# A two-layer trunk on one core: POOL's and PE's side work issued at other places

## The chip, the core and the metric
The kernel runs on one core of a Trainium2 chip. The metric is device time in microseconds (us), median over runs, lower is better. The engines named are PE (TensorE, matrix multiplies), DVE (VectorE), ACT (ScalarE), POOL (GpSimd) and SP (SyncE, which issues all of the DMAs spoken of here). PEld is PE's weight load. L442 means line 442 of the kernel before; where a line of the changed kernel is meant, the text says so.

## The reference
Two layers, sequence 1024, width 1024, float32 in and out. Cut to what matters:

```python
for layer in range(2):
    h = rmsnorm(x, pre_mix_g[layer])
    # layer 0: conformer conv (GLU, width-31 depthwise conv, LayerNorm, swish)
    #          beside an RG-LRU block, joined by one output projection
    # layer 1: mLSTM matrix memory, chunkwise, with a running-max stabiliser
    h = ab_mixer(h, ...) if layer == 0 else mlstm_mixer(h, ...)
    x = x + rmsnorm(h, post_mix_g[layer])
    h = swiglu(rmsnorm(x, pre_ffn_g[layer]), w_gate, w_up, w_down)   # 1024 -> 2816 -> 1024
    x = x + rmsnorm(h, post_ffn_g[layer])
```

## The kernel before
The sequence is held as two halves, A and B, of T = 512 columns. Every product of two float32 matrices is done as three matmuls on high and low parts (`mm3`, L126 to L128); a weight tile `raw` is loaded, cast to its high part on ACT and subtracted to its low part on DVE (`split`, L131 and L132). So a PE step waits for: a load, a cast on ACT, a subtraction on DVE.

The feed-forward part is a Strassen-Winograd scheme over quarters. `phase0` makes the hidden values of half A (blocks `EARLY`, then the last one, `LATE`). `down_first` does the first product of the down projection (`d1`: 11 steps, weight tiles `r20a` in layer 0, `r21a` in layer 1). `phase1` does the gate and up products of both halves jointly over 11 blocks m: for each block it needs joint weights t1 to t4, sums and differences of the raw weight tiles `ri` and `rj`, one set for gate ("g") and one for up ("u"). POOL makes them in `prep1a` (four operations for each kind, L448 to L451; tiles `t14…`, `t23…`), ACT and DVE split them in `prep1b` (`whit2…`, `wlot2…`, and `b22…` for the plain quarter). Before the loop over m, `phase1` also finishes the sums of the activations of half B (`xa…`, `xs…`, `xk…`, L374 to L388, then splits to `xs1…`, `xs2…`, `xa22…`). `down_sums` makes the sums t1 to t4 of the down weights on POOL (11 blocks, four operations and four stores to DRAM each). `phase2` does the six other products of the down projection in the order a12, s4, s2 (with t2), s1 (t1), s3 (t3), a22 (t4).

The order is set by code and a scheduler. Main work (input projections, feed-forward phases) is a generator that `run` walks; at each step it gives other generators, the side work, a number of their own steps: the mixers, `mlstm`, and `sandwich`, which makes the post norm, the residual and the next pre norm of a half. `drain` issues whatever is left of a side generator with no main work between. A tile scheduler then fixes the order on each engine, taking the place in the code as priority. Tile pools bound how far work can get ahead: `raw` has 5 buffers and serves plain weight tiles, `r20a` tiles, `ri` and `rj` alike.

The mixer's part of layer 0 has a LayerNorm whose mean and variance are summed over partitions by one matmul each (`pm`, `pv`, L832, right behind their input sums). `mlstm` walks chunks of 128 tokens; its PE steps in a chunk are `pc` and `pk` (transposes), `sc` (scores), `pn` (numerators, L1060 and L1062, which need `qi` and `pr` from DVE), `pu` (memory update) and `ph` (transposes of the finished rows `nu`). `pgt` transposes the gates once per half.

Around the changed places the trunk reads

```python
run(Project(mb.yT, ob, OUT0).run())
run(f0.phase0(LATE))
run(f0.down_first())
drain(gb)
run(f0.phase1(range(HP)))
```

and the same for layer 1 with `nb`, `f1`. `down_sums` stands whole ahead of the a12 product.

Of the kernel before, what the change touches and what calls it, by code (L numbers as in the profile page):

```python
# [12 lines left out]
OP = mybir.AluOpType  # L13

P = 128
D = 1024
S = 1024
T = 512
NT = 4
# [21 lines left out]
def trunk(ctx: ExitStack, tc: tile.TileContext, x, w_in, w_out, w_gate, w_up, w_down,  # L41
# [18 lines left out]
    def ps_main(name):  # L60
        return pp.tile([P, T], F32, tag="mm", name=name, bufs=4)

    def ps_aux(shape, name):
        return pp.tile(shape, F32, tag="aux", name=name, bufs=4)
# [230 lines left out]
    class Project:  # L295
# [17 lines left out]
        def run(self, before_last=None):  # L313
            self.prep(0)
            for i, c in enumerate(self.chunks):
                last = i == len(self.chunks) - 1
                if last and before_last is not None:
                    before_last()
                self.prep(i)
                yield from accum_out(self.o, self.st, *c, i == 0, last, f"{self.o.name}{c[0]}")  # L320

    HP = NFF // 2
    TT = nc.vector.tensor_tensor

    class Ffn:
# [103 lines left out]
        def prep1(self, m):  # L429
            return self.prep1b(m, *self.prep1a(m))  # L430

        def prep1a(self, m):
            l = self.l
            sub = nc.gpsimd.tensor_tensor
            res = []
            raw = []
            for kind in range(2):
                name = f"{l}{m}{'gu'[kind]}"
                ri = raw_tile([P, D], f"ri{name}")
                rj = raw_tile([P, D], f"rj{name}")  # L440
                src = (w_gate, w_up)[kind]
                nc.sync.dma_start(ri, src[l, m])  # L442
                nc.sync.dma_start(rj, src[l, m + HP])
                u2 = small([P, T], f"u2{name}")
                nc.sync.dma_start(u2, self.d_p[m, kind])
                t23 = unit([P, 2, T], F32, f"t23{name}")
                t14 = unit([P, 2, T], F32, f"t14{name}")
                sub(t14[:, 0], rj[:, 0:T], ri[:, 0:T], op=OP.subtract)  # L448
                sub(t23[:, 0], rj[:, T:], t14[:, 0], op=OP.subtract)
                sub(t23[:, 1], rj[:, T:], rj[:, 0:T], op=OP.subtract)  # L450
                sub(t14[:, 1], ri[:, T:], t23[:, 0], op=OP.subtract)  # L451
                raw.append((rj, t23, t14))
                res.append({"u2": u2})
            for kind in range(2):
                u = unit([P, 2, T], F32R, f"b22{l}{m}{'gu'[kind]}")
                split(u[:, 0], u[:, 1], raw[kind][0][:, T:])
                res[kind]["b22"] = (u[:, 0], u[:, 1])
            return res, raw
# [13 lines left out]
        def phase1(self, ms):  # L472
            l = self.l
            ms = list(ms)
            w_next = self.prep1(ms[0])
            for _ in self.rest:
                pass
            for n, m in enumerate(ms):
                w, h11 = w_next
                u2 = [w[k]["u2"] for k in range(2)]  # L480
                u3, c21, b, c = [], [], [], []
                for k in range(2):
                    a = ps_main(f"pa{l}{m}{k}")
                    self.product(a, w[k]["t2"], self.ops["s2"], True)
                    TT(u2[k], a, u2[k], op=OP.add)
                    yield 2.8
                for k in range(2):
                    b.append(ps_main(f"pb{l}{m}{k}"))
                    self.product(b[k], w[k]["t3"], self.ops["s3"], True)
                    u3.append(small([P, T], f"u3{l}{m}{k}"))  # L490
                    TT(u3[k], b[k], u2[k], op=OP.add)
                    yield 2.8
                if n + 1 < len(ms):
                    w_next = self.prep1(ms[n + 1])
                for k in range(2):
                    c.append(ps_aux([P, T], f"pc{l}{m}{k}"))
                    self.product(c[k], w[k]["t1"], self.ops["s1"], True)
                    TT(u3[k], c[k], u3[k], op=OP.add)
                    yield 2.8
                nc.scalar.activation(u3[0], u3[0], AF.Silu)  # L500
                for k in range(2):
                    self.product(b[k], w[k]["t4"], self.ops["a22"], False)
                    c21.append(small([P, T], f"c21{l}{m}{k}"))
                    TT(c21[k], b[k], u2[k], op=OP.add)
                    yield 2.8
                TT(u3[0], u3[0], u3[1], op=OP.mult)
                nc.sync.dma_start(self.d_s["a22"][m], u3[0])
                nc.scalar.activation(c21[0], c21[0], AF.Silu)
                for k in range(2):
                    self.product(c[k], w[k]["b22"], self.ops["s4"], False)  # L510
                    TT(u2[k], c[k], u2[k], op=OP.add)
                    yield 2.8
                nc.scalar.activation(u2[0], u2[0], AF.Silu)
                TT(c21[0], c21[0], c21[1], op=OP.mult)
                TT(u2[0], u2[0], u2[1], op=OP.mult)
                self.sums(m, h11, u2[0], c21[0], u3[0])
# [77 lines left out]
        def down_first(self):  # L594

            a = [ps_main(f"d1{self.l}{t}") for t in range(NT)]
            for _ in self.down(a, "a11", (0, 0), True):
                yield 2.8
            for t in range(NT):
                f = small([P, T], f"y1{self.l}{t}")  # L600
                nc.scalar.copy(f, a[t])
                nc.sync.dma_start(self.d_y[t], f)

        def phase2(self, oa, ob, by_t=False):
# [3 lines left out]
            lo, hi = slice(0, T), slice(T, 2 * T)  # L608
            ya, yb = oa.y, ob.y
            u2 = [small([P, T], f"v2{l}{t}") for t in range(NT)]  # L610
            for t in range(NT):
                nc.sync.dma_start(u2[t], self.d_y[t])
            for _ in self.down_sums():
                pass
            a = [ps_main(f"d2{l}{t}") for t in range(NT)]
            for _ in self.down(a, "a12", (1, 0), True):
                yield 2.8
            for t in range(NT):
                TT(ya[t][:, lo], a[t], u2[t], op=OP.add)
            b = [ps_aux([P, T], f"d3{l}{t}") for t in range(NT)]  # L620
            for _ in self.down(b, "s4", (1, 1), True):
                yield 2.8
            for t in range(NT):
                nc.scalar.copy(ya[t][:, hi], b[t])  # L624
            a = [ps_main(f"d6{l}{t}") for t in range(NT)]
# [4 lines left out]
            b = [ps_aux([P, T], f"d5{l}{t}") for t in range(NT)]  # L630
            for _ in self.down(b, "s1", "t1", True):
                yield 2.8
            for t in range(NT):
                nc.scalar.copy(yb[t][:, hi], b[t])
                TT(ya[t][:, hi], b[t], ya[t][:, hi], op=OP.add)
                TT(ya[t][:, hi], ya[t][:, hi], u2[t], op=OP.add)
                oa.ready = t
            a = [ps_main(f"d7{l}{t}") for t in range(NT)]
            for _ in self.down(a, "s3", "t3", True):
                yield 2.8  # L640
            for t in range(NT):
                TT(yb[t][:, hi], a[t], yb[t][:, hi], op=OP.add)
                TT(yb[t][:, hi], yb[t][:, hi], u2[t], op=OP.add)
            for t in self.down(a, "a22", "t4", False, by_t):
                if t is not None:
                    TT(yb[t][:, lo], a[t], u2[t], op=OP.add)
# [161 lines left out]
    def conformer(m):  # L808
        h = m.h
        acc = {}  # L810
# [14 lines left out]
        sq = [q[j // 2][:, j % 2] for j in range(4)]  # L825

        def mean(src, tmp, name):
            pm = ps_aux([P, T], name)
            nc.gpsimd.tensor_tensor(tmp[0], src[0], src[1], op=OP.add)
            nc.vector.tensor_tensor(tmp[2], src[2], src[3], op=OP.add)  # L830
            nc.vector.tensor_tensor(tmp[0], tmp[0], tmp[2], op=OP.add)
            nc.tensor.matmul(pm, onesl, tmp[0], start=True, stop=True)  # L832
            return pm

        pm = mean(acc, sq, f"pm{h}")
        yield
        for j in range(4):
            nc.vector.tensor_tensor(acc[j], acc[j], pm, op=OP.subtract)
            nc.scalar.activation(sq[j], acc[j], AF.Square)
            yield  # L840
        pv = mean(sq, sq, f"pv{h}")
        yield
        rs = sq[3]
        nc.scalar.activation(rs, pv, AF.Sqrt, bias=epsc)
        nc.vector.reciprocal(rs, rs)
# [108 lines left out]
    def mlstm(m):  # L954
        h = m.h
# [6 lines left out]
        nc.scalar.activation(e, e, AF.Exp, scale=-1.0)  # L962
        log1p_exp(l, e, [P, NT, 8], "mg")
        nc.vector.scalar_tensor_tensor(gi[:, :, 32:40], gf, 0.0, l, op0=OP.min, op1=OP.subtract)
        yield
        yield
        pg = ps_aux([P, T], f"pgt{h}")
        for t in range(NT):
            nc.tensor.transpose(pg[0:40, t * P:(t + 1) * P], gi[:, t], ident)
# [36 lines left out]
        for c in range(NT):  # L1006
# [44 lines left out]
            for s in range(2):  # L1051
                nc.vector.tensor_tensor(prv[:, s], scs[s], ewv[:, s], op=OP.mult)
                yield
            yield
            va = unit([P, 8, 128], F32, f"nu{h}{c}")
            den = sp.tile([P, 8], F32, tag="den", name=f"den{h}{c}", bufs=2)
            for i in range(4):
# [166 lines left out]
    ob = Out("oB")  # L1224
    gb = start(sandwich(ob, x, x1, post_mix[0:1], 1, gf(0), f0.feature_b, 6), 1.0)
    run(Project(mb.yT, ob, OUT0).run())
    run(f0.phase0(LATE))
    run(f0.down_first())
    drain(gb)
# [22 lines left out]
    pb = Out("pB")  # L1252
    gb = start(sandwich(pb, x2, x3, post_mix[1:2], 1, gf(1), f1.feature_b, 6), 1.0)
    run(Project(nb.yT, pb, OUT1).run())
    run(f1.phase0(LATE))
    run(f1.down_first())
    drain(gb)
# [96 lines left out]
```

## Time and profile before
| what | us |
|---|---|
| median of 3 runs | 2136.77 (2134.54 to 2140.83) |
| the profiled execution, device time | 2129.51 |
| its span on the core | 2127.7 |
| PE busy in it | 2049.7 |
| DVE busy | 1455.5 |
| ACT busy | 925.9 |
| POOL busy | 704.7 |

The busy time of PE is 96% of the span, so nearly all that can be gained by order alone lies in the time in which PE idles or runs at a lower granted clock. The mean granted clock over the span is 0.990 of full speed. The lists of waits name, for each idle time of an engine, the instruction that ended it; the tables by stretch give busy time, granted clock (PEclk, 1.00 is the upper level) and the share of the DMA engines in use.

### The profile page before, as it was taken

The numbers are of one execution on the slowest core, as the hardware profiler recorded it, in microseconds if no ns is written. First come the engines' busy times: TensorE is split into PE (matmuls) and PEld (weight loads), VectorE is DVE, ScalarE is ACT, GpSimd is POOL, SyncE is SP. The second block draws the span as 40 slices with busy tenths as digits, with TensorE's granted clock in tenths as the row PEclk, the third lists the DMA queues.
The fourth block names the chain that finished last, engine by engine and source line by source line (L and its number), as shares of the span: only waits on it lengthen the run. The fifth ranks groups of instructions, "written<-read, shape, count | busy, mean of one in ns | idle before, by whom it ended". The sixth has DMA issues, their size and how long they took to land.

```text
span 2127.7 us, 26147 instructions
## 1 busy us (share of the span) xinstructions
PE 2049.7 (96%) x9200; PEld 1669.0 (78%) x9200; DVE 1455.5 (68%) x2017; ACT 925.9 (44%) x1313; POOL 704.7 (33%) x473
## 2 busy tenths in 40 slices
PE   7998989997999999999999999999997999999998
PEld 6776867785888887878988887778885888888786
DVE  7998479569677776567643755556469877777567
ACT  5666477654222222445343334555454222223353
POOL 4454554627444336401000000300016643445310
PEclk9999999998999999999999999999998999999999
DMA  6232544475454459966563653756464545469966
GB/s 229 92 117 81 182 163 163 144 248 187 164 167 160 168 201 366 342 203 229 190 208 118 219 180 99 257 179 213 134 223 176 192 167 168 165 214 367 327 225 220
DMA packets 202740, 417.39 MB, mean 196 GB/s; under 512 B 19920, under 2 KB 48720, under 8 KB 202608
## 3 DMA queue, kind: packets, MB, share of 16 engines
q1 hardware_dynamic: 202608, 415.72, 57.2%
q8 instruction: 72, 1.18, 0.2%
q14 instruction: 60, 0.49, 0.1%
HBM read 302.82 MB, written 112.82 MB: 195 GB/s over the span
## 4 chain that ended last, share of the span: by engine, by line
PE 67%; DVE 13%; DMA 9%; issue 6%; ACT 4%; POOL 1%; SPq 1%; DVEq 0%; POOLq 0%; ACTq 0%
PE pb L128 4%; PE pb L126 4%; PE pb L127 4%; PE pc L128 3%; PE pc L126 3%; PE pc L127 3%; DVE pcv L754 3%; PE d L126 3%; PE d L127 3%; PE d L128 3%; PE p L126 3%; PE p L127 3%; PE p L128 3%; DMA ft<-wt 2%; PE pa L128 2%
## 5 line engine op out<-in xcount | busy, mean ns | idle before, releaser
L107 ACT CAST whi<-raw 128x1024 fp32r<-128x1024 f32 (+2 forms) x164 | 164.3, 1006 | 244.2 <-PE p L127 50.0
L109 POOL TENSOR_TENSOR wlo<-raw,whi 128x1024 fp32r<-128x1024 f32 x66 | 162.0, 2461 | 165.8 <-ACT whi L107 126.5
L109 DVE TENSOR_TENSOR wlo<-raw,whi 128x1024 fp32r<-128x1024 f32 (+2 forms) x98 | 111.7, 1145 | 123.7 <-ACT whi L107 122.8
L754 DVE SCALAR_TENSOR_TENSOR pcv<-cy,vec,pcv 128x512 f32<-128x512 f32 x240 | 172.1, 749 | 4.4 <-ACT pcv L751 1.6
L1091 POOL TENSOR_TENSOR hrr<-hss,half 128x8 f32<-128x8 f32 x8 | 13.1, 1643 | 243.7 <-DVE hss L1089 243.7
L132 DVE TENSOR_TENSOR wlod1s<-r21s,whid1s 128x1024 fp32r<-128x1024 f32 x44 | 58.5, 1334 | 46.4 <-ACT whid1s L131 46.0
L132 DVE TENSOR_TENSOR wlod0s<-r20s,whid0s 128x1024 fp32r<-128x1024 f32 x44 | 57.6, 1310 | 44.0 <-ACT whid0s L131 39.8
L126 PE MATMUL p<-xTnoA,whi 128*128 128x512 f32 x176 | 71.8, 412 | 6.2 <-ACT gel L729 2.6
L131 ACT CAST whid1s<-r21s 128x1024 fp32r<-128x1024 f32 x44 | 46.4, 1054 | 66.7 <-PE d L128 38.0
L131 ACT CAST whid0s<-r20s 128x1024 fp32r<-128x1024 f32 x44 | 46.4, 1054 | 61.3 <-PE d L128 49.0
L127 PE MATMUL d<-wlod0s,whid0s 128*128 128x512 f32 x176 | 69.2, 393 | 2.0 <-DVE wlod0s L132 2.0
L126 PE MATMUL p<-xTnpA,whi 128*128 128x512 f32 x176 | 70.9, 405 | 0.0
L127 PE MATMUL p<-xTnoA,whi 128*128 128x512 f32 x176 | 70.3, 400 | 0.0
L128 PE MATMUL p<-xTnpA,wlo 128*128 128x512 f32 x176 | 70.3, 401 | 0.0
L127 PE MATMUL p<-xTnpA,whi 128*128 128x512 f32 x176 | 70.1, 399 | 0.0
L128 PE MATMUL p<-xTnoA,wlo 128*128 128x512 f32 x176 | 69.8, 400 | 0.0
L128 PE MATMUL d<-whid1s,wlod1s 128*128 128x512 f32 x176 | 69.1, 393 | 0.0
L127 PE MATMUL d<-wlod1s,whid1s 128*128 128x512 f32 x176 | 69.0, 392 | 0.0
L128 PE MATMUL d<-whid0s,wlod0s 128*128 128x512 f32 x176 | 68.6, 390 | 0.0
L126 PE MATMUL d<-whid1s 128*128 128x512 f32 x176 | 63.1, 394 | 3.1 <-ACT yeA L624 3.1
L132 DVE TENSOR_TENSOR wlod0a<-r20a,whid0a 128x1024 fp32r<-128x1024 f32 x33 | 47.3, 1440 | 25.3 <-ACT whid0a L131 23.8
L548 POOL TENSOR_TENSOR wt<-wq 128x512 f32<-128x512 f32 x22 | 34.7, 1575 | 89.0 <-DMA wq<-in_w_down 49.6
(2484 smaller groups left out, 6640.8 us busy)
## 6 DMA issues: line engine op xcount, KB each, us to landing
wq<-in_w_down SPq DMA_DIRECT2D x88, 256.0 KB, 5.1
ft<-wt SPq DMA_DIRECT2D x88, 256.0 KB, 5.1
raw<-in_w_in SPq DMA_DIRECT2D x32, 512.0 KB, 3.4
raw<-in_m_in SPq DMA_DIRECT2D x32, 512.0 KB, 4.9
raw<-in_w_gate SPq DMA_DIRECT2D x22, 512.0 KB, 4.5
raw<-in_w_up SPq DMA_DIRECT2D x22, 512.0 KB, 3.6
fp<-p1f SPq DMA_DIRECT2D x44, 256.0 KB, 2.5
fs<-s SPq DMA_DIRECT2D x44, 256.0 KB, 3.5
```

Source lines behind the costliest of these rows:

```text
L107: nc.scalar.copy(hi[:, 0:n], raw[:, 0:n])
L109: eng.tensor_tensor(lo[:, 0:n], raw[:, 0:n], hi[:, 0:n].bitcast(F32), op=OP.subtract)
L126: nc.tensor.matmul(ps, l[0], r[0], start=first, stop=False, **kw)
L127: nc.tensor.matmul(ps, l[0], r[1], start=False, stop=False, **kw)
L128: nc.tensor.matmul(ps, l[1], r[0], start=False, stop=last, **kw)
L131: nc.scalar.copy(dst_hi, src)
L132: nc.vector.tensor_tensor(dst_lo, src, dst_hi.bitcast(F32), op=OP.subtract)
L548: sub(t[0][:, 0], q[0][:, 1], q[0][:, 0], op=OP.subtract)
L754: nc.vector.scalar_tensor_tensor(dst, src[:, k:k + T], V(wname, w0 + k), dst, op0=OP.mult, op1=OP.add)
L1091: nc.gpsimd.tensor_tensor(rr, ss, half, op=OP.pow)
```

## The change
Five edits, all of order:

1. `prep1a` can be called for one kind at a time and continue an earlier call. The gate kind of block 0 is issued ahead of `phase0(LATE)`, the up kind at the start of `down_first`; `phase1` goes on from there.
2. `down_sums` runs one block with every second step of the a12 and s4 products, and the rest behind them.
3. In the LayerNorm the matmul comes four side steps later than its input.
4. In `mlstm`, `pgt` comes two side steps later, and the numerators of each chunk two later.
5. In `phase2` four additions on half B stand ahead of the s3 product, not behind it.

```diff
-        def prep1a(self, m):
+        def prep1a(self, m, kinds=(0, 1), begun=None):
             l = self.l
             sub = nc.gpsimd.tensor_tensor
-            res = []
-            raw = []
-            for kind in range(2):
+            res, raw = begun or ([], [])
+            for kind in kinds:
                 name = f"{l}{m}{'gu'[kind]}"
...
                 res.append({"u2": u2})
-            for kind in range(2):
                 u = unit([P, 2, T], F32R, f"b22{l}{m}{'gu'[kind]}")
                 split(u[:, 0], u[:, 1], raw[kind][0][:, T:])
                 res[kind]["b22"] = (u[:, 0], u[:, 1])
...
         def phase1(self, ms):
-            w_next = self.prep1(ms[0])
+            w_next = self.prep1b(ms[0], *self.begun)
...
         def down_first(self):
             a = [ps_main(f"d1{self.l}{t}") for t in range(NT)]
+            self.begun = self.prep1a(0, (1,), self.begun)
...
-            for _ in self.down_sums():
-                pass
+            sums = self.down_sums()
             a = [ps_main(f"d2{l}{t}") for t in range(NT)]
-            for _ in self.down(a, "a12", (1, 0), True):
+            for i, _ in enumerate(self.down(a, "a12", (1, 0), True)):
+                if i % 2 == 0:
+                    next(sums, None)
                 yield 2.8
...
-            for _ in self.down(b, "s4", (1, 1), True):
+            for i, _ in enumerate(self.down(b, "s4", (1, 1), True)):
+                if i % 2 == 0 or i == 9:
+                    next(sums, None)
                 yield 2.8
+            for _ in sums:
+                pass
...
+            for t in range(NT):
+                TT(yb[t][:, hi], yb[t][:, hi], u2[t], op=OP.add)
             a = [ps_main(f"d7{l}{t}") for t in range(NT)]
             for _ in self.down(a, "s3", "t3", True):
                 yield 2.8
             for t in range(NT):
                 TT(yb[t][:, hi], a[t], yb[t][:, hi], op=OP.add)
-                TT(yb[t][:, hi], yb[t][:, hi], u2[t], op=OP.add)
...
         def mean(src, tmp, name):
-            pm = ps_aux([P, T], name)
...
+            for _ in range(4):
+                yield
+            pm = ps_aux([P, T], name)
             nc.tensor.matmul(pm, onesl, tmp[0], start=True, stop=True)
+            yield
...
         nc.vector.scalar_tensor_tensor(gi[:, :, 32:40], gf, 0.0, l, op0=OP.min, op1=OP.subtract)
-        yield
-        yield
+        for _ in range(4):
+            yield
         pg = ps_aux([P, T], f"pgt{h}")
...
-            yield
+            for _ in range(3):
+                yield
             va = unit([P, 8, 128], F32, f"nu{h}{c}")
...
+    f0.begun = f0.prep1a(0, (0,))
     run(f0.phase0(LATE))
...
+    f1.begun = f1.prep1a(0, (0,))
     run(f1.phase0(LATE))
```

The joint start of layer 0 on POOL. `srnoB` and `srpoB` are single numbers per row that the sandwich of half B needs (an inverse root each); the `t14` and `t23` tiles are the first block's joint weights. Before:

```order
L147 TENSOR_TENSOR srnoB_3548<-svnoB_3546,half 128x1
L147 TENSOR_TENSOR srpoB_3558<-svpoB_3556,half 128x1
L147 TENSOR_TENSOR srnoB_3582<-svnoB_3580,half 128x1
L147 TENSOR_TENSOR srpoB_3592<-svpoB_3590,half 128x1
L147 TENSOR_TENSOR srnoB_3630<-svnoB_3628,half 128x1
L448 TENSOR_TENSOR t1400g<-rj00g,ri00g 128x512
L450 TENSOR_TENSOR t2300g<-rj00g 128x512
```

and of the change:

```order
L147 TENSOR_TENSOR srnoB_3548<-svnoB_3546,half 128x1
L147 TENSOR_TENSOR srpoB_3558<-svpoB_3556,half 128x1
L447 TENSOR_TENSOR t1400g<-rj00g,ri00g 128x512
L449 TENSOR_TENSOR t2300g<-rj00g 128x512
L448 TENSOR_TENSOR t2300g<-rj00g,t1400g 128x512
L147 TENSOR_TENSOR srnoB_3582<-svnoB_3580,half 128x1
L147 TENSOR_TENSOR srpoB_3592<-svpoB_3590,half 128x1
L450 TENSOR_TENSOR t1400g<-ri00g,t2300g 128x512
L147 TENSOR_TENSOR srnoB_3645<-svnoB_3643,half 128x1
L447 TENSOR_TENSOR t1400u<-rj00u,ri00u 128x512
```

Three of the gate kind's operations now stand in front of the last two pairs of the sandwich's inverse roots; the up kind's follow directly behind these.

The same stretch in SP's queue of DMA issues: `ri00g` to `rj00u` are the four raw tiles of the first joint block, `r20a` those of `d1`. Before, these four stand behind `d1`'s loads:

```order
L374 DMA xknoB_3728<-fx_223 128x512
L561 DMA r20a_3983<-fa_226 128x512
L565 DMA r20a_3983<-in_w_down 128x512
L374 DMA xanoB_3777<-fx_223 128x512
L442 DMA ri00g<-in_w_gate 128x1024
L374 DMA xknoB_3775<-fx_223 128x512
L443 DMA rj00g<-in_w_gate 128x1024
L374 DMA xanoB_3824<-fx_223 128x512
L442 DMA ri00u<-in_w_up 128x1024
L374 DMA xknoB_3822<-fx_223 128x512
L443 DMA rj00u<-in_w_up 128x1024
```

and of the change:

```order
L441 DMA ri00g<-in_w_gate 128x1024
L442 DMA rj00g<-in_w_gate 128x1024
L105 DMA raw_3610<-in_m_g 128x544
L105 DMA raw_3616<-in_m_g 128x544
L441 DMA ri00u<-in_w_up 128x1024
L217 DMA x_115<-xroB_3267 128x1024
L158 DMA xroB_3517<-in_x 128x1024
L442 DMA rj00u<-in_w_up 128x1024
L217 DMA x_115<-xroB_3517 128x1024
L158 DMA xroB_3551<-in_x 128x1024
L415 DMA fp_225<-p1f_3635 128x512
L559 DMA r20a_3739<-fa_226 128x512
```

The four loads have gone from the end of `d1`'s loads to the front of the first one.

DVE in layer 0's `phase2`, where the s1 product ends (`d` into `yfA`, then `v` added) and the s3 product begins (`wlod0s` is the low part of one of its weight tiles). Before:

```order
L635 TENSOR_TENSOR yfA_6316<-d_7163,yfA_6316 128x512
L635 TENSOR_TENSOR yfA_6317<-d_7164,yfA_6317 128x512
L635 TENSOR_TENSOR yfA_6318<-d_7165,yfA_6318 128x512
L636 TENSOR_TENSOR yfA_6316<-yfA_6316,v_6324 128x512
L635 TENSOR_TENSOR yfA_6319<-d_7166,yfA_6319 128x512
L636 TENSOR_TENSOR yfA_6317<-yfA_6317,v_6325 128x512
L636 TENSOR_TENSOR yfA_6318<-yfA_6318,v_6326 128x512
L132 TENSOR_TENSOR wlod0s_7425<-r20s_7421,whid0s_7424 128x1024
```

and of the change:

```order
L639 TENSOR_TENSOR yfA_6316<-d_7163,yfA_6316 128x512
L643 TENSOR_TENSOR yfB_6320<-yfB_6320,v_6324 128x512
L639 TENSOR_TENSOR yfA_6317<-d_7164,yfA_6317 128x512
L643 TENSOR_TENSOR yfB_6321<-yfB_6321,v_6325 128x512
L639 TENSOR_TENSOR yfA_6318<-d_7165,yfA_6318 128x512
L643 TENSOR_TENSOR yfB_6322<-yfB_6322,v_6326 128x512
L640 TENSOR_TENSOR yfA_6316<-yfA_6316,v_6324 128x512
L639 TENSOR_TENSOR yfA_6319<-d_7166,yfA_6319 128x512
L643 TENSOR_TENSOR yfB_6323<-yfB_6323,v_6327 128x512
L640 TENSOR_TENSOR yfA_6317<-yfA_6317,v_6325 128x512
L132 TENSOR_TENSOR wlod0s_7429<-r20s_7425,whid0s_7428 128x1024
```

Ten operations stand ahead of the weight's subtraction in place of seven.

PE at the end of `mlstm` of half A: the last numerators `pn`, the memory update `pu`, the last transposes `ph`, and the output projection `popA`. Before, 31 main matmuls (`pimo`) stand between the last `pn` and `ph`, the last of them here:

```order
L127 MATMUL pimo_10429<-xTnfB_8426,whi_10241 128x512
L128 MATMUL pimo_10429<-xTnfB_8426,wlo_10242 128x512
L126 MATMUL pimo_10429<-xTnfB_8434,whi_10241 128x512
L127 MATMUL pimo_10429<-xTnfB_8434,whi_10241 128x512
L128 MATMUL pimo_10429<-xTnfB_8434,wlo_10242 128x512
L1103 MATMUL ph_10371<-ident,nu_10302 128x128 x4
L1103 MATMUL ph_10380<-ident,nu_10302 128x128 x4
L126 MATMUL popA_10485<-whi_10391,yspA_10457 128x512
```

and of the change:

```order
L1067 MATMUL pn_10322<-cst,qi_10282 128x258
L1069 MATMUL pn_10322<-vt_10212,pr_10299 128x129 x2
L1078 MATMUL pu_10328<-vt_10212,kw_10287 128x258
L1078 MATMUL pu_10332<-vt_10212,kw_10287 128x258
L1078 MATMUL pu_10336<-vt_10212,kw_10287 128x258
L1078 MATMUL pu_10340<-vt_10212,kw_10287 128x258
L1110 MATMUL ph_10371<-ident,nu_10302 128x128 x4
L1110 MATMUL ph_10380<-ident,nu_10302 128x128 x4
L126 MATMUL popA_10485<-whi_10391,yspA_10457 128x512
```

The numerators, the update and the transposes now stand together behind the last of the main matmuls.

## Rows read from the trace of the kernel before

**Rows 1.** The page's head: span, and PE's busy time.

```profile
span 2127.7 us, 26147 instructions
PE 2049.7 (96%) x9200; PEld 1669.0 (78%) x9200; DVE 1455.5 (68%) x2017; ACT 925.9 (44%) x1313; POOL 704.7 (33%) x473
```

**Rows 2.** PE's waits, whole span: us in total, times, longest us.

```profile
PE pa L126 <- ACT whit210g L131: 9.2, 1, 9.2
PE d L127 <- DVE wlod0a L132: 8.5, 5, 4.8
PE pv L832 <- DVE lnq L831: 4.0, 1, 4.0
PE d L126 <- ACT yeA L624: 3.1, 1, 3.1
...
PE pn L1060 <- DVE qi L1035: 2.6, 1, 2.6
PE pn L1062 <- DVE pr L1052: 2.6, 2, 1.5
...
PE d L127 <- DVE wlod0s L132: 2.0, 2, 1.4
...
PE d L126 <- DVE yfA L619: 1.3, 1, 1.3
...
PE ph L1103 <- DVE nu L1093: 1.1, 1, 1.1
```

**Rows 3.** Stretches around layer 0's joint start: busy us, granted clock, DMA.

```profile
450.00:460.00 10.00, 10.00 (x49) 8.24 (x48) 8.11 (x11) 6.32 (x9) 2.80 (x3) 1.00 0.99 337
460.00:470.00 10.00, 10.00 (x52) 8.35 (x51) 7.19 (x9) 8.40 (x12) 0.55 (x1) 1.00 1.00 370
470.00:480.00 10.00, 10.00 (x50) 8.23 (x49) 9.33 (x14) 6.33 (x9) 0.00 (x0) 1.00 0.75 251
480.00:490.00 10.00, 6.69 (x29) 4.91 (x27) 9.97 (x9) 3.72 (x5) 8.56 (x5) 0.96 0.39 135
490.00:500.00 10.00, 5.27 (x12) 3.43 (x13) 9.69 (x9) 6.29 (x12) 5.91 (x4) 0.67 0.69 234
500.00:510.00 10.00, 7.18 (x19) 5.31 (x19) 10.00 (x14) 6.17 (x12) 5.84 (x3) 0.69 0.60 214
```

**Rows 4.** DVE in order of time, 476 to 494: start, us, line, tiles.

```profile
478.82 1.22 DVE L132 TENSOR_TENSOR wlod0a<-r20a,whid0a 128x1024 fp32r<-128x1024 f32 x1
...
485.23 1.77 DVE L132 TENSOR_TENSOR xs2noB<-xanoB,xs2noB 128x512 fp32r<-128x512 f32 x1
486.93 0.68 DVE L132 TENSOR_TENSOR xs3noB<-xbnoB,xs3noB 128x512 fp32r<-128x512 f32 x1
...
489.20 2.28 DVE L132 TENSOR_TENSOR wlod0a<-r20a,whid0a 128x1024 fp32r<-128x1024 f32 x1
```

**Rows 5.** POOL in order of time: first and last operation of block 0.

```profile
480.70 1.83 POOL L448 TENSOR_TENSOR t1400g<-rj00g,ri00g 128x512 f32<-128x512 f32 x1 [18.76 <-DMA rj00g<-in_w_gate]
...
494.38 1.60 POOL L451 TENSOR_TENSOR t1400u<-ri00u,t2300u 128x512 f32<-128x512 f32 x1
```

**Rows 6.** Stretches around layer 1's joint start, columns as in rows 3.

```profile
1610.00:1620.00 10.00, 0.80 (x4) 0.38 (x3) 9.17 (x12) 6.05 (x11) 2.43 (x2) 0.78 0.37 130
1620.00:1630.00 10.00, 7.63 (x19) 5.07 (x20) 10.00 (x15) 9.82 (x17) 3.23 (x2) 0.67 0.75 269
1630.00:1640.00 10.00, 9.52 (x36) 7.29 (x36) 10.00 (x6) 2.19 (x3) 10.00 (x6) 0.87 0.00 0
```

**Rows 7.** Stretches in layer 0's down projection, columns as in rows 3.

```profile
820.00:840.00 20.00, 16.71 (x66) 12.95 (x65) 12.24 (x8) 5.78 (x6) 11.60 (x8) 0.91 1.05 404
840.00:860.00 20.00, 20.00 (x90) 16.56 (x89) 9.45 (x8) 7.38 (x7) 11.79 (x8) 1.00 1.05 395
```

**Rows 8.** DVE at the end of half A's mLSTM, in order of time.

```profile
1276.75 0.16 DVE L1065 COPY den<-pn 128x2 f32<-128x2 f32 x1 [0.41 <-ACT nu L1064]
...
1284.84 1.23 DVE L1093 TENSOR_TENSOR nu<-nu,hrr 128x1024 f32<-128x1024 f32 x1 [0.37 <-POOL hrr L1091]
```

More of the change, by code (lines that the diff above doesn't have):

```diff
@@ L831, in mean @@
             nc.vector.tensor_tensor(tmp[0], tmp[0], tmp[2], op=OP.add)
+            for _ in range(4):
+                yield
+            pm = ps_aux([P, T], name)
             nc.tensor.matmul(pm, onesl, tmp[0], start=True, stop=True)
+            yield
             return pm
-        pm = mean(acc, sq, f"pm{h}")
-        yield
+        pm = yield from mean(acc, sq, f"pm{h}")
         for j in range(4):
@@ L840, in conformer @@
             yield
-        pv = mean(sq, sq, f"pv{h}")
-        yield
+        pv = yield from mean(sq, sq, f"pv{h}")
         rs = sq[3]
@@ L964, in mlstm @@
         nc.vector.scalar_tensor_tensor(gi[:, :, 32:40], gf, 0.0, l, op0=OP.min, op1=OP.subtract)
-        yield
-        yield
+        for _ in range(4):
+            yield
         pg = ps_aux([P, T], f"pgt{h}")
@@ L1053, in mlstm @@
                 yield
-            yield
+            for _ in range(3):
+                yield
             va = unit([P, 8, 128], F32, f"nu{h}{c}")
```

## The prediction

> **What bounds the kernel now.** I read the page's head first, then PE's list of waits over the whole span, then tables by stretch around the longest waits, then DVE and POOL there in order of time. PE is busy 2049.7 of 2127.7 us [rows 1]. So a change of order alone can give back at most the 78 us in which PE idles, and what a lower granted clock costs beside it. The list of waits shows that nearly every idle time ends on DVE or ACT, that is on a split of a weight tile or a vector step, not on a DMA or on POOL directly [rows 2].
>
> The two largest places are the joint starts, where the first joint products `pa` begin. In layer 0, between 480 and 510, PE is busy 6.69, 5.27 and 7.18 us at granted clocks of 0.96, 0.67 and 0.69 [rows 3]. Busy time by clock is 6.4 + 3.5 + 5.0 = 14.9 us of full-speed work in 30, so 15.1 us are lost. In layer 1, between 1610 and 1640, it is 0.80, 7.63 and 9.52 at 0.78, 0.67 and 0.87 [rows 6], 14.0 in 30, so 16.0 are lost. In both DVE is 92 to 100% busy: it is the chain there, first with half B's activation sums and the `d1` weights, then with the joint weights' low parts.
>
> Why DVE is late is seen from its rows in order of time. A subtraction of 128x1024 takes 1.22 us at 478.82 and 2.28 at 489.20; one of 128x512 takes 0.68 at 486.93 and 1.77 at 485.23 [rows 4]. The long ones lie between 480.70 and 496, where POOL makes block 0's eight joint sums [rows 5]; there are eight long ones, two of the large kind and six of the small. So POOL's work costs DVE 8 x 1.05 = 8.4 us at the one place where DVE holds up PE.
>
> **The change, part by part.** The profiled run took 2129.51 us for its span of 2127.7, and the sum is made against it. The median shown is 2136.77, 7.3 above it. I take the differences as the same for both and quote the forecast on the median.
>
> Joint weights, layer 0. No instruction is added. The four raw tiles are issued ahead of all `d1` loads, and POOL makes the gate sums between the sandwich's inverse roots, the up sums right behind. I put them between 455 and 472. DVE idles there for 1.9 + 2.8 = 4.7 us in 450 to 470 and 0.7 in the next ten [rows 3], so of the 8.4 some 4.7 are taken in by idle time and up to 3.7 push the chain; 4.7 are saved. The `b22` splits, two of 0.60 (a row's start to the next one's [rows 4]), leave the chain: 1.2. In the new order the last low part (up kind, t2 and t3) stands one activation split and one set-2 subtraction earlier: about 1.8. Together 7.7, taken as 8. Ends: 3 (only the last two terms) and 11 (no push at all). Its price: the sandwich's last roots queue behind POOL sums that wait for `rj00g`, and the raw tiles hold four of five raw buffers, so that `d1`'s first steps come late, between 457 and 464. I expect a PE wait of some 4 us there, but the joint start hangs on DVE and not on `d1`, so it only moves a wait that stands at 486 now.
>
> Joint weights, layer 1. The same edit. The POOL sums stand just before the start there too, with as many long DVE steps; PE's wait is 9.2 us in one piece [rows 2]. DVE has more room before it than in layer 0, so I take 9; ends 4 and 12.
>
> Down sums, layer 0. Before, the sums' loads stand in SP's queue ahead of the a12 product's weight tiles. Of the five waits of `d` for `wlod0a` [rows 2], two (3.3 us) lie in 820 to 840, where the clock is 0.91 of PE's 16.71 busy us: 15.2 of 20, so 4.8 lost [rows 7]. With the sums spread over two products the weight loads come first. I take 4 of the 4.8. The DMA engines are at 1.05 there and in the next stretch, so the bytes don't get fewer; the last sums' stores come later, and the s2 product, which reads t2, may wait in their place. Ends 0 and 4.8. Four `yfA` additions also stand earlier on DVE; the wait of 1.3 for them [rows 2] I count as 1 saved, 0 to 1.3.
>
> The same in layer 1: the wait of 3.1 for `yeA` copies on ACT [rows 2] lies where the s2 product starts, behind the sums. The order now has the first casts for that product ahead of those copies, but its loads come later. I take 2 saved; ends -2 and +4.
>
> Additions moved ahead of the s3 product. DVE has ten additions before a weight's low part in place of seven: 3 x 0.60 = 1.8 us later, where PE already waits 1.4, the longest of the two for `wlod0s` [rows 2]. The wait grows to 3.2, with a part of a slower clock: 2.5 lost, 0 to 3.5. In layer 1 there is no wait now at that place: 1 lost, 0 to 1.8. The additions that go from behind the product cost nothing there.
>
> LayerNorm matmuls. Behind the change `pm` of half A stands at the same main matmul as before and its wait stays; `pv` stands four main matmuls later. At 49 to 52 matmuls in 10 us [rows 3] that is 0.8 of its wait of 4.0 [rows 2]; 0.9 taken, 0 to 1.5.
>
> mLSTM, in its chunks. `pn` waited 2.6 in total in half A (two waits) and 2.6 in half B (one wait, for `qi`) [rows 2]. In half B nine main matmuls come in between: 9 x 0.2 = 1.8, taken as 1.9. In half A one of the two waits goes, 1.5.
>
> mLSTM, end of half A. Here the same edit costs. The steps that were moved back run out of main work: 31 `pimo` matmuls, some 7 us, stood between the last `pn` and `ph`, now none. From the last numerators (DVE copies the last denominator at 1276.75) to the end of `nu` (1284.84 + 1.23) it takes 9.3 us [rows 8], with squares and copies on ACT and one root on POOL between, of which some 3 are other work on ACT; so 6.3. The four `pu` in front of `ph` cover about 1.2. I expect a wait of 5 where 1.1 stands now [rows 2], and 1.7 for a lower clock, as the stretch with 3.3 us of waits at 820 lost 4.8: net 5.6 lost, ends 3 and 9. Half B's end has 35 main matmuls behind its last `pn` and does not wait.
>
> Sum: 8 + 9 + 4 + 1 + 2 - 2.5 - 1 + 0.9 + 1.9 + 1.5 - 5.6 = 19.2 us saved. The profiled run would be 2110; on the median 2136.8 - 19.2 = 2118.
>
> **The rivals.**
>
> First, the contention only moves. What speaks for it: DVE is already 72 to 93% busy in 450 to 480 [rows 3], and it works there on the same chain. Then the saving of the joint starts falls to the order terms, about 3 in each layer. The sum is 19.2 - 5 - 6 = 8; with the sums' DMAs given back at the s2 product (the 4 gone and 1 more lost) it is 3, 2134. Against it: in layer 1 the stretch before the start has idle time on DVE. The long steps beside POOL show a price of 1.05 each [rows 4], and nothing in the rows says that it is less elsewhere. The Trainium skill's "SBUF — State Buffer" (section "Who interferes with whom") states an exclusive lock on a port pair that VectorE shares with GpSimd, under which the loser is blocked for a whole instruction. By that rule POOL's eight sums cost DVE the same wherever they run, which is this rival; the rows agree that the price is one per POOL operation.
>
> Second, the other side: `d1` starves. The place is the raw pool: the joint block's four tiles hold four of five buffers from before `phase0(LATE)` on, until POOL and both `b22` splits have read them, and each `d1` step then waits for load, cast and split one after another on the fifth. A wait of `d` for `wlod0a` costs 1.7 on average and 4.8 at most [rows 2]; with the clock, say 3.3. The kernel becomes slower by more than the bound when 25.6 us are lost on it, 8 of the 22 `d1` steps in two layers. That happens if the last roots and the sums wait for each other, so that POOL's set ends as late as now. With ten steps, 33 us, it takes 2136.8 - 19.2 + 33 = 2151; with eight 2143. Against it: the issues stand 40 places earlier, and POOL is idle for 18.76 us before its first sum [rows 5], so it should be done by 472.
>
> Third, the joint starts are freed completely: 15.1 and 16.0 in place of 8 and 9. This gives 19.2 + 14.1 = 33, so 2103. Against it: DVE still has the splits of `xs1`, `xa22` and `xs4` and block 1's sums at the start, both of which stay.
>
> **How the numbers follow.** Of the measurement about 0.3%, 6.4 us, can be told from no change: below 2130.4 is faster, above 2143.2 slower. The forecast, between 2108 and 2130, gets 0.60. The first rival gets 0.17, mostly within 0.3%. The full freeing gets 0.13. The starvation gets 0.10. Faster is 0.60 + 0.13 + 0.02 of the first rival = 0.75, the same 0.15, slower 0.10. The range runs from 2102, the full freeing, to 2137, which takes in the first rival and leaves out starvation; its low end leaves out little.
>
> **What would show it.** In the profile after: POOL's eight sums of block 0 ended before 475 and before 1595, DVE's steps between 480 and 500 at 0.68 and 1.22; waits of `pa` at both joint starts adding to less than half; a new `d` wait around 460 that costs nothing at the joint start. The a12 waits are gone; the first s3 wait is about 3; `ph` waits about 5 at the end of half A's mLSTM. It is wrong if `pa` waits as long as now while POOL is done early (then DVE was not late through POOL), or if `d` waits grow by more than 20 us.

## The result and the profile after

The changed kernel takes 2123.8 us (median, 2121.0 to 2124.7) against 2137.2 before: ratio 0.9936, 95% interval 0.9921 to 0.9951. A second measurement, beside the last experiments, gave 2123.4 against 2135.2, ratio 0.9949 (0.9937 to 0.9962). So 12 to 13 us were gained where 19 had been forecast.

The page's head of the kernel after; PE's busy time is as in [rows 1]:

```profile
span 2122.4 us, 26145 instructions
PE 2049.3 (97%) x9200; PEld 1667.5 (79%) x9200; DVE 1470.3 (69%) x2017; ACT 925.6 (44%) x1314; POOL 718.8 (34%) x473
```

PE's waits of the kernel after, over the whole span (us in total, times, longest), cut to the longest that the change bears on, to be set against [rows 2]:

```profile
...
PE pa L126 <- ACT y L600: 7.4, 2, 5.7
PE pm L839 <- DVE lnq L835: 6.3, 1, 6.3
PE ph L1110 <- DVE nu L1100: 6.0, 1, 6.0
PE d L127 <- DVE wlod0s L132: 3.7, 2, 3.2
PE pb L126 <- DVE u L489: 3.6, 2, 2.7
PE d L126 <- ACT whid0s L131: 3.3, 2, 3.0
PE d L127 <- DVE wlod0a L132: 3.0, 2, 2.6
PE d L126 <- ACT whid0a L131: 2.9, 1, 2.9
...
```

The waits of `pa` on joint weights are gone, and the 3.1 for `yeA` too. New are: `pa` waits for the copies `y` of `d1`'s results on ACT, `d` waits in `d1` (for `whid0a`, and 2.6 for `wlod0a`), `d` waits for `whid0s` where the s2 product starts, `pb` waits for `u`, and `ph` waits 6.0. The 6.3 of `pm` is chance and not the change (first experiment). The wait at the s3 product has grown from 1.4 to 3.2.

Stretches around layer 0's joint start in the kernel after (columns as in rows 3):

```profile
450.00:460.00 10.00, 8.54 (x41) 6.55 (x40) 7.62 (x10) 6.04 (x11) 7.69 (x5) 1.00 0.92 308
460.00:470.00 10.00, 5.92 (x22) 4.68 (x23) 7.89 (x7) 6.16 (x8) 7.46 (x7) 0.83 0.85 310
470.00:480.00 10.00, 9.68 (x48) 7.69 (x47) 9.90 (x11) 6.56 (x10) 3.88 (x3) 1.00 0.71 242
480.00:490.00 10.00, 10.00 (x47) 8.32 (x46) 9.90 (x14) 6.46 (x10) 0.00 (x0) 1.00 0.94 334
490.00:500.00 10.00, 8.80 (x39) 6.89 (x37) 9.80 (x13) 6.89 (x11) 1.49 (x1) 1.00 0.77 271
500.00:510.00 10.00, 5.54 (x18) 4.43 (x19) 10.00 (x16) 8.46 (x16) 3.89 (x2) 0.66 0.29 107
```

Against [rows 3], PE is now nearly full from 480 to 500, but 450 to 470, which was full, has lost 5.5 us of PE's time, and a sixth of the clock in its second half. DVE idles 4.5 us there now, where it idled 4.7. DVE and POOL there, in order of time:

```profile
455.32 2.32 DVE L140 SCALAR_TENSOR_TENSOR junkpoB<-yoB 128x1024 bf16<-128x1024 f32 x1
...
457.68 2.19 DVE L214 TENSOR_TENSOR yoB<-yoB,groB 128x1024 f32<-128x1024 f32 x1
...
466.84 4.28 DVE L132 TENSOR_TENSOR wlod0a<-r20a,whid0a 128x1024 fp32r<-128x1024 f32 x2 [0.89 <-ACT whid0a L131]
471.04 1.77 DVE L382 TENSOR_TENSOR xsnoB<-xbnoB,xknoB 128x512 f32<-128x512 f32 x1
```

```profile
453.01 1.30 POOL L447 TENSOR_TENSOR t1400g<-rj00g,ri00g 128x512 f32<-128x512 f32 x1
...
472.34 1.62 POOL L450 TENSOR_TENSOR t1400u<-ri00u,t2300u 128x512 f32<-128x512 f32 x1
```

POOL is done at 474, as forecast (472). The long DVE steps of [rows 4] have moved with it: 2.2 to 2.3 for a step of 1.22, 1.77 for one of 0.68.

To see the gain place by place, each main matmul that uses a low part was found in both traces, and its start in the first was taken from its start in the second (median over the 40 us from the time named). This difference is what "by position" means from here on. Between second traces of both kernels (below), the changed kernel is later (+) or earlier (-), in us:

```
at (before)      400    440   480    520   760   840   880   920   960   1240   1280   1480  1560  1600   1640   1960  2000   2080
after - before  -0.3   +8.6  +5.4   -3.3  -2.8  -9.3  -8.9  -3.6  -2.0   -5.8   +1.7   -1.3  +0.5  +4.4   -4.3   -4.5  -9.7   -8.0
```

So layer 0's joint start gained 3.0 in all, the a12 product 6.5, of which 5.3 are given back at 910 and 1.6 more lost to 960; half A's mLSTM first gains 3.8 and then loses 7.5; layer 1's joint start gains 4.8 and its s2 product 5.2. The first two traces give 3.2, 4.9, 5.0 back, 2.1 lost, 4.3 and 8.3, 5.4 and 5.0 for the same places. The differences from 0 to 400 and within 2 us behind 1300 are of the size of chance: two traces of the kernel before differ by up to 2.8 at one place, at 840. The table ends at 8.0, and these two executions are 7.5 apart (2133.65 and 2126.14, the slowest of its five): 4 to 5 us of the gain of the medians are in no pair of traces.

### The profile page after: what moved, and what is told of

Its sections match the earlier page's. It is cut to its first block, busy times and chain, and to the rows that moved or that the text cites. A ratio compares the mean times of both kernels' runs of the same rounds, so it can differ in the third digit from the quotient of the medians.

```text
span 2122.4 us, 26145 instructions
## 1 busy us (share of the span) xinstructions
PE 2049.3 (97%) x9200; PEld 1667.5 (79%) x9200; DVE 1470.3 (69%) x2017; ACT 925.6 (44%) x1314; POOL 718.8 (34%) x473
## 5 line engine op out<-in xcount | busy, mean ns | idle before, releaser
L131 ACT CAST whid1s<-r21s 128x1024 fp32r<-128x1024 f32 x44 | 46.1, 1055 | 65.0 <-PE d L128 41.6
```

Of the source, the lines that this page charges most:

```text
L131: nc.scalar.copy(dst_hi, src)
```

## The experiments

**The kernel before, again** (no edit).

> The kernel before, unchanged, for a second trace of it. Theory: the first trace of it (2129.51 us, 7 below its median) is a lucky one, and the two traces of before and after differ at the LayerNorm for a reason that isn't the change: in the trace after, DVE is already 4.25 us late at 110 us, where the orders are still the same, through two steps that met a POOL operation (a copy of 0.15 us that took 2.41, a scan of 1.21 that took 3.11). Then a second trace of before is some 4 to 8 us longer than the first, with waits at other places (pm near 6 us, not 2.73), and the median again near 2137. Rival: the traces of before are alike within 1 us, and the 13.4 us of the medians lie in stretches that the two traces show.

Measured: 2134.21 against 2134.44, ratio 1.000 (0.9991 to 1.0009); the profiled run took 2133.65. The first trace, 2129.51, was a lucky one. `pm` waits 2.73 in it and 6.30 in the second trace, and about 6.3 in 12 of the 14 traces of this study, whatever the kernel. What goes with it is one copy at 85 us. In the first trace, on DVE and POOL:

```profile
84.85 0.15 DVE L725 COPY cr<-rec 128x3 f32<-128x3 f32 x1
```

```profile
84.84 2.43 POOL L109 TENSOR_TENSOR wlo<-raw,whi 128x1024 fp32r<-128x1024 f32 x1 [3.02 <-ACT whi L107]
```

In the second trace of before (the second of these two copies):

```profile
84.87 0.16 DVE L725 COPY cr<-rec 128x3 f32<-128x3 f32 x1
85.01 2.40 DVE L725 COPY cr<-rec 128x3 f32<-128x3 f32 x1
```

```profile
84.98 2.39 POOL L109 TENSOR_TENSOR wlo<-raw,whi 128x1024 fp32r<-128x1024 f32 x1 [3.01 <-ACT whi L107]
```

In the second trace the copy stood as long as POOL's whole step; a scan at 107.6 then took 3.11 in place of 1.21, and DVE is 3.7 us late up to the LayerNorm. The copy is held, the scan long and `pm` near 6.3 in the same 12 traces; the two others (the first of before, and a_gate's) have none of the three. With it PE is by position 2.0 us later at 200 and 0.5 at 280, so it is a part of the difference between the two traces, 4.1 us, and not all of it: 2.8 more come at 840, from other waits in the a12 product.

**The joint edit undone** in the changed kernel.

```diff
...
-            w_next = self.prep1b(ms[0], *self.begun)
+            w_next = self.prep1(ms[0])
...
-            self.begun = self.prep1a(0, (1,), self.begun)
...
-    f0.begun = f0.prep1a(0, (0,))
...
-    f1.begun = f1.prep1a(0, (0,))
```

> The changed kernel with the joint weights' edit undone, the rest kept. By the forecast's terms (8 + 9) it is 17 us slower than the changed kernel, near 2141. By PE's position in the two traces, 3.2 us were gained across layer 0's joint start and 5.4 across layer 1's: 8.6 slower, near 2132. By the rival in which the contention only moves: under 3 slower.

Measured: 2134.14, ratio 0.9997 (0.9987 to 1.0007), some 10 us slower than the changed kernel: near the 8.6 taken from the positions, and neither 17 nor under 3. By position it is 8.2 us earlier than the changed kernel from 400 to 480 and then 12.3 later across the start (net 4.1); in layer 1, 4.3 earlier and then 9.7 later (net 5.4).

**POOL's sums of block 0 left out** of the kernel before. The splits read the raw tiles in their place, so this kernel computes something else.

```diff
+                if m == 0:
+                    t23 = ri.rearrange("p (a b) -> p a b", b=T)
+                    t14 = rj.rearrange("p (a b) -> p a b", b=T)
+                else:
...
```

> The kernel before, with POOL's eight joint sums of block 0 left out in both layers (the splits read the raw tiles in their place). It measures what these sums cost DVE and PE where the kernel before has them. By the forecast's reading (DVE is the chain, 8 long steps at 1.05 us each) each joint start ends 8 us earlier and PE with it: 16 us faster than before, near 2118, DVE's steps at 1.22 and 0.68 there. By the rival that DVE's time isn't all of the wait (the chain of d1 and of ACT stands right behind): 4 to 6 us per layer, 2123 to 2126.

Measured: 2120.49, ratio 0.9927 (0.9915 to 0.9939), 15 us faster; by position 7.5 at layer 0's start and 7.8 at layer 1's. The price of 8 that the forecast read from the rows was right, though the run takes away the splits' wait for POOL as well.

The edit doesn't save that price, it pays it elsewhere. In all traces of both kernels DVE has the same 50 steps between its last subtraction for a 128x544 tile, near 448, and its first for `xs1noB`, near 500 (without the sums one more, of some 1.2 us). That stretch in before_again, after, after_again and b_nopool, columns as in rows 3, DVE's busy time being the third (a step cut by an edge of the stretch counts in its x):

```profile
447.48:500.82 53.34, 44.56 (x204) 35.35 (x203) 45.60 (x50) 36.54 (x55) 18.92 (x13) 0.96 0.78 267
```

```profile
449.02:500.63 51.61, 43.91 (x199) 34.94 (x197) 45.74 (x51) 33.70 (x49) 20.69 (x14) 0.97 0.83 290
```

```profile
447.44:499.54 52.10, 45.26 (x198) 36.00 (x196) 45.26 (x51) 33.60 (x49) 20.22 (x14) 0.93 0.85 287
```

```profile
448.39:495.24 46.85, 46.85 (x223) 38.57 (x222) 38.48 (x52) 35.73 (x53) 4.61 (x5) 1.00 0.88 289
```

DVE is as busy with the sums moved as before, and 7 us less without them. In the seven traces that have both kinds early and these 50 steps it is busy 44.2 to 45.7 and idle 5.9 to 7.4; in the three with the sums at the start 45.6 to 45.8 and 7.6 to 7.8. So the move shortens DVE's way to the joint start by 1.1 to 2.4 us.

**Only the gate kind early.**

```diff
-            self.begun = self.prep1a(0, (1,), self.begun)
...
-            w_next = self.prep1b(ms[0], *self.begun)
+            w_next = self.prep1b(ms[0], *self.prep1a(0, (1,), self.begun))
```

> The changed kernel with only the gate kind's joint weights ahead of d1; the up kind is again made at the start of phase1. It tells apart why d1 waits at 458 to 464 (2.64 and 2.90 us, and a slower clock: 8.2 us by PE's position against the kernel without the joint edit). Theory: the four raw tiles hold four of five raw buffers and d1's tiles come one at a time; with two held, those waits fall to under 2 in all, while the up kind's four sums cost DVE 4 x 1.05 at the joint start: 4 faster in layer 0, about 0 in layer 1, so 2 to 5 faster than the changed kernel. Rival: d1 waits because POOL's sums delay the sandwich and DVE, not for buffers: the waits stay and the kernel is 4 to 8 slower.

Measured: 2127.46, ratio 0.9969 (0.9957 to 0.9980), 4 slower than the changed kernel. The stretch where `d1` starved, with two raw buffers held in place of four:

```profile
450.00:460.00 10.00, 8.47 (x38) 6.33 (x37) 9.35 (x10) 5.05 (x7) 7.64 (x6) 1.00 0.83 294
460.00:470.00 10.00, 10.00 (x49) 7.71 (x48) 8.01 (x9) 8.15 (x11) 2.10 (x2) 1.00 0.92 333
...
500.00:510.00 10.00, 5.67 (x15) 4.53 (x16) 9.55 (x14) 5.71 (x11) 5.44 (x2) 0.66 0.25 96
```

PE is full from 460 on, 6.3 us earlier by 480 than with both kinds early, and the waits of `d` from 440 to 480 are 1.4 in place of 5.9. That it is the buffers, and not only POOL's work, which is halved here too, is seen in the kernel after from the first four loads of `d1`, in SP's queue:

```profile
450.10 0.42 SPq L559 DMA_DIRECT2D r20a<-fa  x1
...
461.15 0.33 SPq L559 DMA_DIRECT2D r20a<-fa  x1
...
462.54 0.36 SPq L559 DMA_DIRECT2D r20a<-fa  x1
...
463.53 0.42 SPq L559 DMA_DIRECT2D r20a<-fa  x1
```

and from what DVE and POOL do there:

```profile
459.92 1.21 DVE L132 TENSOR_TENSOR wlod0a<-r20a,whid0a 128x1024 fp32r<-128x1024 f32 x1
...
461.65 0.68 DVE L132 TENSOR_TENSOR b2200g<-rj00g,b2200g 128x512 fp32r<-128x512 f32 x1
```

```profile
462.02 1.47 POOL L450 TENSOR_TENSOR t1400g<-ri00g,t2300g 128x512 f32<-128x512 f32 x1
```

The second load goes out as the first tile's subtraction ends (461.13), the third 0.2 behind the end of the split of `rj00g` (462.33), the fourth as POOL is done with `ri00g` (463.49): each waits for a buffer. In a_gate six such loads are out by 461, in a_nojoint seven.

What was expected of the total was wrong: the up kind's sums at the start cost 6.0 to 6.5 in layer 0, which takes back what `d1` gained there, and 6.9 to 7.5 in layer 1, not 4.2, through waits for `whit200u` and `whit210u`:

```profile
PE pa L126 <- ACT whit210u L131: 6.8, 1, 6.8
PE pa L126 <- ACT whit200u L131: 6.3, 1, 6.3
```

**The copies of `d1`'s results on DVE.**

```diff
-                nc.scalar.copy(f, a[t])
+                nc.vector.tensor_copy(f, a[t])
```

> The changed kernel with the copies of the d1 product's results made by DVE in place of ACT. In the trace after, pa waits 5.66 us in layer 0 and 1.70 in layer 1 for these copies, which give pa its bank and stand on ACT behind the casts of xs1, xa22 and xs4 (from 498.1 to 503.8). If that queue is the new wait at the joint start, the copies come about 4 us earlier and cost DVE 4 x 0.6: 2 to 5 us faster than the changed kernel, 2119 to 2122. Rival: DVE is still the chain, and its 2.4 us more per layer make it 3 slower.

Measured: 2124.05, ratio 0.9945 (0.9932 to 0.9957): no difference from the changed kernel. In layer 0 the wait of 5.7 becomes one of 3.3 for `whit200u`, in layer 1 that of 1.7 becomes one of 4.8 for the copies themselves. So the place of the copies in ACT's queue is not what sets the start by itself; DVE, busy 9.8 to 10.0 of each 10 us from 470 to 510 in the kernel after, has 2.4 us more to do here.

**Down sums whole again.**

```diff
-            sums = self.down_sums()
+            for _ in self.down_sums():
+                pass
...
```

> The changed kernel with the down sums again whole ahead of the a12 product, the rest kept. By the traces layer 0 gains 5.0 us before 880 and loses 5.0 at 900, where the s2 product begins, and layer 1 gains 3: undone, 3 us slower than the changed kernel, with waits for wlod0a at 820 to 840 and none at 900. By the forecast (4 + 1 + 2) 7 slower. If what is given back at 900 is the whole, 0.

Measured: 2137.73, ratio 1.0014 (1.0005 to 1.0023), 14 slower than the changed kernel; none of the expectations. PE's waits:

```profile
PE d L127 <- DVE wlod0a L132: 5.7, 4, 2.6
...
PE d L126 <- DVE yfA L618: 4.2, 1, 4.2
PE d L126 <- DVE yeA L618: 3.9, 1, 3.9
```

By position 13.6 are lost up to 880, 5.0 come back at 910, 1.8 go at 960; layer 1 loses some 2.5 at its joint start and 4.1 at s2. The waits of 5.7 and 3.9 are near those of before (4.8 to 8.5, and 3.1 to 3.3). The 4.2 for `yfA`, 1.3 or less in the kernel before, has a reason in DVE's order: the four additions stand behind 13 subtractions `wlod0s` here and behind 12 there, and PE waits from 878.5 while the thirteenth runs from 879.6 to 881.9. So the run isn't quite the old order, and 14 is more than the sums' edit is worth against the kernel before. What remains of the 7 us by which it exceeds the pair of traces stays open.

**The four additions back behind the s3 product.**

```diff
-            for t in range(NT):
-                TT(yb[t][:, hi], yb[t][:, hi], u2[t], op=OP.add)
             a = [ps_main(f"d7{l}{t}") for t in range(NT)]
...
                 TT(yb[t][:, hi], a[t], yb[t][:, hi], op=OP.add)
+                TT(yb[t][:, hi], yb[t][:, hi], u2[t], op=OP.add)
```

> The changed kernel with the four additions on half B again behind the s3 product. By the traces (a wait of 3.20 in place of 1.39, 2.5 us by PE's position in layer 0, none in layer 1): 2.5 faster than the changed kernel, near 2121.5. By the forecast (2.5 and 1): 3.5 faster. Rival: the additions then hold up the next product as before, 0 to 1.

Measured: 2122.11, ratio 0.9938 (0.9925 to 0.9951). The interval can't tell it from the changed kernel. By position 2.2 are gained between 940 and 960 and nothing in layer 1, and the wait is 1.4 again.

**mLSTM's later steps undone in half A.**

```diff
-        for _ in range(4):
+        for _ in range(2 if h == 0 else 4):
...
-            for _ in range(3):
+            for _ in range(1 if h == 0 else 3):
```

> The changed kernel with the mLSTM's later steps undone in half A only (half B keeps them). By PE's position in the traces half A's chunks gained 4.7 us by the edit and its end lost 9.2: undone, 4.5 faster than the changed kernel, near 2119.5, with a ph wait of 1.1 again. By the forecast (1.5 gained, 5.6 lost) 4 faster. Rival: the wait at the end comes back at popA or in half B, and nothing is gained.

Measured: 2120.80, ratio 0.9929 (0.9917 to 0.9941), 3 faster by the medians, with intervals that overlap; by position 4.7 later in the chunks and 9.2 earlier at the end, net 4.5, as expected. `ph` in the changed kernel, and in this one:

```profile
1290.98 1.94 PE L1110 MATMUL ph<-ident,nu 128*128 128x128 f32 x8 [6.02 <-DVE nu L1100]
```

```profile
1287.69 1.06 PE L1110 MATMUL ph<-ident,nu 128*128 128x128 f32 x8 [1.01 <-DVE nu L1100]
```

After the long wait the same eight matmuls take 1.94 in place of 1.06, at a lower clock: from 1290 to 1300 the granted clock is 0.70 in the changed kernel and 1.00 here.

**More main work ahead of the end of half A's mLSTM.** The weight stream hands out tiles in a fixed order, so here two projections are computed with each other's weights.

```diff
-    run(gb, 32)
+    run(gb, 36)
     drain(sa)
-    run(gb, 2)
```

> The changed kernel with four more steps of half B's input projection issued ahead of the end of half A's mLSTM (36 in place of 32 and 2 behind), so that 24 main matmuls stand between its last numerators and the memory update, and as many before it. By the theory that the tail lost 9.2 us by PE's position (a wait of 6.0 and a slower clock) the time falls by 7 to 9, to 2115 to 2117. Rival: the chain through DVE and POOL only moves on to popA, and the time falls by less than 2.

Measured: 2122.09, ratio 0.9941 (0.9927 to 0.9954), under 2 faster by the medians, and not told from the changed kernel by the interval. The `ph` wait goes, but `popA` waits 3.0 for `yspA`. By position 1.4 to 1.6 are gained up to 1360, and 1.2 to 1.3 given back by 1440, where half B has less main work now: the rival was right.

**The changed kernel again, and two combinations.** `best1` is a_h0 with a_noadds; `best2` has a_gate's edit as well.

> The changed kernel, unchanged, on the chip of the runs beside it: 11 to 14 us faster than before, ratio 0.9935 to 0.9950. By PE's position in a second trace of each, layer 0's joint start gains about 4 and layer 1's about 5.

> The changed kernel with the mLSTM's later steps undone in half A and the four additions again behind the s3 product. By the traces 4.5 + 2.2 = 6.7 faster than the changed kernel, near 2117; by the medians of the two edits alone (3.0 and 1.7) 4.7, near 2119. The ratio to before is 0.9900 to 0.9925.

> The same two edits, and only the gate kind's joint weights ahead of d1. If the theory on the raw buffers holds, 2 to 5 faster than the version without it, 2112 to 2117; by the rival 4 to 8 slower than that, 2121 to 2127.

Measured side by side: 2123.42, 2119.10 and 2119.24, ratios 0.9949, 0.9922 (0.9908 to 0.9936) and 0.9930 (0.9917 to 0.9942). best1 is 4 faster than the changed kernel by the medians, as the sum of the two edits' medians had it, and beats both kernels. best2 is the same as best1; neither expectation on it holds. So a_gate's edit cost 4 by itself and nothing here. By position it costs 0.2 in layer 0 and 3.4 in layer 1 here too, and 3.9 come back between 880 and 960, for a reason that stays open.

## Why the prediction was right in its sign and too large in its size

*Joint starts (forecast 8 and 9; measured 3.0 and 4.8 by position in one pair, 4.1 and 5.4 against a_nojoint).* The reading of the rows was right: the sums cost DVE 8 us a layer at the start (b_nopool 7.5 and 7.8). The signs that the prediction named came as well: POOL is done at 474 and 1595, and `pa` waits 8.4 us in all in place of 19.4. The failing step is the term "of the 8.4 some 4.7 are taken in by idle time". In layer 0 DVE is busy as long as before on its way to the start, 45.3 to 45.7 us against 45.6 to 45.8, and its idle time there shrinks by 0.8 to 2.0 only. Between 452 and 467 it still waits 1.15 us for a load and 1.22 and 0.89 for ACT, though POOL's sums now run there. The `b22` splits, counted as 1.2 saved, are among these steps in both kernels. What was gained beside that is order: the low part `wlot200u` begins at 507.3, and at 512.2 in a_nojoint, where layer 0 begins 0.6 earlier. So the first rival, that the contention only moves and some 3 a layer are left, had the mechanism right and nearly the size. In layer 1 it is much the same: DVE is busy 45.2 to 45.5 us up to the same step, three steps of 1.2 that now stand ahead of it taken off (an estimate), and 46.1 to 46.3 before.

The wait in `d1` was forecast at some 4 us, as one that only moves. It came as 5.5 with a slower clock behind it, 8.2 by position. Whether it delayed the start isn't shown: in a_gate `d1` is not held up and the start is no earlier, but there the up kind's sums stand at the start.

*Down sums (4 + 1 + 2).* In layer 0 the a12 waits went, 4.9 to 6.5 us where 5 was forecast, but 5.0 to 5.3 came back where the s2 product starts, as the prediction had feared and not counted: between 900 and 920 PE is busy 16.95 of 20 in the trace after, and 20.00 before. Layer 1 gained 5.0 to 5.2, not 2. Together 4.9 to 6.4 in the pairs: that this is near the forecast's 7 is luck, as the parts were wrong. Undoing the edit costs 14, some 3 of it by another order on DVE.

*Additions (-2.5 and -1).* 2.2 lost in layer 0, none in layer 1; the wait is 3.2, as forecast.

*LayerNorm (0.9).* `pv` waits 1.48 in before_again and 1.14 in after_again, so about 0.3 of it, beside chance of several us at the same place; the 4.0 of [rows 2] was that of the lucky trace. No run undid this edit by itself.

*mLSTM (+1.5 - 5.6 in half A, +1.9 in half B).* The end's wait was 6.0 (forecast 5), and its whole cost 7.5 to 9.2, as the lower clock cost more than 1.7: PE's 8.77 busy us from 1290 to 1300 at a clock of 0.70 are 2.6 us by themselves (an estimate). The chunks gained 3.8 to 4.7. Net 3.7 to 4.5 lost, against 4.1. Half B gained 1.1 in the pair, within chance, and was not undone by itself.

The rival of starvation had the right place and mechanism and the wrong size: two waits in layer 0 and one in layer 1, not eight steps.

The single edits don't add up: undone one by one they are worth 10 and 14, and -3 and -2, which is 19 and not 12 to 13.

## What to carry to other kernels

POOL work that costs DVE time at a DVE-bound start cost it the same where it was moved to; idle time counted there is no gain as long as DVE waits there for something else (4.7 us were counted, 1 to 2 were used). And its tiles hold buffers that the work in between needs. Side work moved later must still have main work behind it at the end of its stage. And before two traces are compared line by line, a second trace of the same kernel shows which lines belong to chance.

## What was not expected of the hardware

A DVE copy of 128x3, 0.15 us by itself, took 2.40 when it began 0.03 us behind a POOL step of 2.39. That agrees with the Trainium skill's "SBUF — State Buffer" (section "Who interferes with whom"), by which the loser of the shared port pair waits for a whole instruction. In the two traces in which it wasn't held, the same copy began 0.01 and 0.02 us behind such a step, the two smallest distances of the 14; the held ones began 0.02 to 0.04 behind. The price shows much later: 3.7 us on DVE from 110 us on, and a wait of PE for the LayerNorm that is 3.6 us longer, of which 2.0 are left by position at 200.
